# A decoder layer on one core: one activation half's low part moved to an aligned place, small parameters loaded in transposed form, and one chunk's matmuls in plain order

## The chip, the cores and the metric

The kernel runs on one core of one Trainium2 chip. The metric is device time in microseconds (us) of one execution. The engines spoken of are PE (TensorE: matmuls and transposes; PEld is its weight load), ACT (ScalarE), DVE (VectorE), POOL (GpSimd) and SP (SyncE, which here only issues DMAs). Each engine works through its own queue in order; a `behind(...)` in the code only sets where an instruction stands in a queue.

## The reference

One layer of 512 tokens and 1024 columns, float32: half a step of a SwiGLU feed-forward network (FFN1), a token mixer, and half a step of a second one (FFN2), each between two RMS norms:

```
x = x + 0.5 * rms_norm(swiglu_ffn(rms_norm(x, norm_pre[l, 0]), ffn1_w_in[l], ffn1_w_out[l]), norm_post[l, 0])
mixed = token_mixer(rms_norm(x, norm_pre[l, 1]), w_mix_in[l], conv_w[l], conv_b[l],
                    mlstm_gate_bias[l], lower_bounds[l], hgrn_norm[l], mlstm_norm[l], w_mix_out[l])
x = x + rms_norm(mixed, norm_post[l, 1])
x = x + 0.5 * rms_norm(swiglu_ffn(rms_norm(x, norm_pre[l, 2]), ffn2_w_in[l], ffn2_w_out[l]), norm_post[l, 2])
```

`swiglu_ffn` is `(silu(gate) * up) @ w_out` with `gate, up = split(x @ w_in)` and 2816 inner columns. The mixer projects to the inputs of four HGRN2 heads and four mLSTM heads, puts the mLSTM queries and keys through a causal convolution of width 4 (`conv_w`, `conv_b`), runs both recurrences in chunks, norms each head (`hgrn_norm`, `mlstm_norm`) and projects back. `lower_bounds` is the running sum of a softmax over `hgrn_lb_logits`.

## The kernel before, in words

**Precision.** A float32 operand is split in two parts of type fp32r: `hi`, a rounding made on ACT (L289 for weights), and `lo`, the rest, made on DVE (L291). Each product of two operands is three matmuls: hi with hi, hi with lo, lo with hi.

**First matrix of the FFNs.** The 11 pairs of column blocks are each computed from seven products p1 to p7 of half-size operands (a Strassen scheme with shared sums), written out by hand as the lists `HEADS`, `ORDER`, `HEADS2` and `ORDER2`; pair 0 of FFN1 goes by eight plain products c1 to c4 and e1 to e4. A product (`prod`, L621) is 24 matmuls of 128x128 by 128x256. p2 accumulates into the PSUM bank in which p1 stands, after ACT has copied p1's result out of it (L648); p2's matmuls into the bank wait for that copy. What follows a product on ACT or DVE stands in `after`.

**The activation tiles.** The transposed, split activations stand in four tiles `xt[0]` to `xt[3]` (their fp32r views are `xq[n]` or `xh[n]`), each with hi first and lo behind it. In `xt[0]` the lo part that the FFN's products p1, c1 and c3 read stands 16 elements (64 B, `STEP`) off the aligned place `D:2*D`. The sums of activations for p3, p6 and p7 (tiles `sq`) are made in the FFN's head by the steps L392 and L393 (the "turns"), on DVE and ACT in turn.

**The start.** `start` lists the first products of FFN1 and the splits and turns between them, and `small_params` loads the convolution's weights and bias, the logits and the two head norms: five DMAs from SP into 36 rows of a tile `rows` (L1273 to L1277), one PE transpose (L1279), one DVE copy into the tile `prm` (L1280, 128 partitions x 36), and then the softmax for the lower bounds on DVE and ACT (L1283 to L1293, with a table load on ACT at L1286).

**The end of FFN1.** `ffn_out` multiplies by the second matrix chunk by chunk of 128 tokens; the last of the four chunks has an order of its own, which lets one weight place go early ("free") so that the first mixer weight is split (`first_split`) in the middle of the chunk. `head4` then begins the mixer's projection (L561, L550).

Of the kernel before, what the change touches and what calls it, by code (L numbers as in the profile page):

```python
# [118 lines left out]
class Layer:  # L119
# [146 lines left out]
    def split(self):  # L266

        nc = self.nc
        it = self.items.popleft()
        raw = self.raw[it.key]  # L270
        _, a, b = raw.shape
        if it.dst:
            w = it.dst()
        else:
            if self.wt is None:
                self.wt = self.wp.tile([P, 2 * D * WBUF + FRONT + PAD], F32R, name="w")
            if not self.slot and it.key[0] != "mix":
                self.free = deque(FREE2 if it.key[0] == "f2" else FREE)
            n, o = self.lie("out" if it.key[1] == "out" else "mix" if it.key[0] == "mix" and b == 512 else "any")
            self.free.remove(n)  # L280
            w = self.wt[:, o : o + 2 * D].rearrange("p (b k t) -> p b k t", b=2, k=a)
            self.slot[id(w)] = n, o, w
        hi, lo = self.both(w)
        if it.sums:
            raw, hi, lo = (self.flat(v)[:, QUARTER:] for v in (raw, hi, lo))
        self.ready.append((w, it.dst is not None))
        rows = it.rows
        if rows is None:
            self.cast = nc.scalar.copy(hi, raw)  # L289
            yield  # L290
            self.low = nc.vector.tensor_tensor(lo, raw, hi.bitcast(F32), op=ALU.subtract)  # L291
        else:
            for j in range(a):
                nc.scalar.activation(hi[:, j], raw[:, j], AF.Copy, scale=rows[:, j : j + 1])
            yield
            for j in range(a):
                nc.vector.scalar_tensor_tensor(
                    lo[:, j], raw[:, j], rows[:, j : j + 1], hi[:, j].bitcast(F32), op0=ALU.mult, op1=ALU.subtract
                )
        with self.behind(*self.hold):  # L300
            for out, other in it.adds:
# [3 lines left out]
                added = (nc.vector if late else nc.gpsimd).tensor_tensor(o, o, c, op=ALU.add)  # L305
# [206 lines left out]
                stack.enter_context(self.tc.issue_after(i.ins))  # L512
            yield

    def last(self, mm, ys, pieces, g, after, trans, head, out=lambda i: (), cast=False):


        for i in range(NT):
            for left in mm(i):
                if left == "free":  # L520
                    self.first_split = self.split()
                    next(self.first_split)
                    with self.behind(self.cast):
                        after(i - 1)
                elif i == NT - 1 and left == 2:
                    trans(i - 2)
            self.post1(i, *ys[i], pieces(i), g, *out(i))
            if not (cast and i == 2):
                after(i)
            if i == 2:  # L530
                trans(0)
        head(trans)
# [32 lines left out]
    def head4(self, trans, scaled):  # L565
# [2 lines left out]

        self.head = []
        lows = [self.low]  # L570
        for _ in self.first_split:
            pass
        with self.behind(*lows, self.low):
            scaled(2, 0)
        with self.behind(self.added[0]):
# [13 lines left out]
    def open_ffn(self, ctx, second=False):  # L589
# [12 lines left out]
        self.left.update({"e1": xq[2], "e2": xq[3], "e3": xq[2], "e4": xq[3]})  # L602
        self.gs, self.held, self.copies = [], {}, []
        self.hs, self.bank, self.later, self.u, self.had = deque(), {}, deque(), {}, set()

    def prod(self, p, t, feed=True):

# [28 lines left out]
    def after(self, p, t):  # L636
# [23 lines left out]
                gate()  # L660
        elif p == "p5" and t < self.filled:
            u = self.u[t] = self.st("u")
            tt(self.two_by(u), self.two_by(bank["p5", t]), h1, ALU.subtract)
        elif p == "p5":
            q = bank["p6", t] = self.ps()
            tt(self.two_by(q), self.two_by(bank["p5", t]), h1, ALU.subtract)
# [29 lines left out]
    def ffn_head(self, trans):  # L696
# [13 lines left out]
        for n, (p, t) in enumerate(HEADS2):  # L710
# [6 lines left out]
            if n == 0:  # L717
                with self.behind(*norm):
                    trans(2)
            elif n == 2:  # L720
                trans(3)
            elif n in (5, 6, 8, 9):
                for g in self.gs:
                    next(g)
        self.hold = ()
        self.holes()

# [10 lines left out]
    def start(self, gpre):  # L738
# [84 lines left out]
        p12 = prod()  # L823
        e2()
        self.full_split()
        step(g2)
        step(g3)
        p21 = prod()
# [16 lines left out]
    def ffn_in(self):  # L845
# [5 lines left out]
        for n, (p, t) in enumerate(ORDER2[len(HEADS2) :] if self.second else ORDER[len(HEADS) :]):  # L851
# [11 lines left out]
            self.after(p, t)  # L863
            if t == PAIRS - 1 and p in ("p3", "p7"):
                self.hs.append(self.h_tile(len(self.hs)))
        self.feed()
        self.lag()

# [95 lines left out]
    def ffn_out(self, gpost_row, scale, after, trans, head):  # L964
# [140 lines left out]
        def chunk(i):  # L1105
            vn = [(v, n) for v in range(2) for n in range(LF)]
            if i == 0:

                vn.sort(key=lambda f: f[1])
            turns = [(v, LF - 1) for v in range(2)]  # L1110
            if i == NT - 1 and not self.second:

                vn.insert(1, vn.pop(LF))
                turns[0] = vn[LF - 1]
            for v, n in vn:
                plain(C, ws[n], hs[n], i, v, False)
# [9 lines left out]
        self.last(chunk, ys, lambda i: pieces(C, i), g, after, trans, head, lambda i: (self.hf[:, 4 + i, :],), not self.second)  # L1126
        self.holes()


# [135 lines left out]
                    made.append(Item((name, PAIRS - 1, "a"), ()))  # L1265
        return made

    def small_params(self):

        nc = self.nc  # L1270
        mc = self.cp
        rows = self.sp.tile([36, P], F32, tag="junk", bufs=1, name="rows")
        nc.sync.dma_start(rows[0:16, :], self.conv_w[0].rearrange("j (c p) -> (j c) p", p=P))  # L1273
        nc.sync.dma_start(rows[16:20, :], self.conv_b[0].rearrange("(c p) -> c p", p=P))
        nc.sync.dma_start(rows[20:28, :], self.hgrn_lb_logits.rearrange("r (c p) -> (r c) p", p=P))
        nc.sync.dma_start(rows[28:32, :], self.hgrn_norm[0].rearrange("(c p) -> c p", p=P))
        nc.sync.dma_start(rows[32:36, :], self.mlstm_norm[0].rearrange("(c p) -> c p", p=P))  # L1277
        pt = self.ps()
        nc.tensor.transpose(pt[:, :36], rows, self.ident[:36, :36])  # L1279
# [3 lines left out]
        nc.vector.tensor_tensor(mx, l0, l1, op=ALU.max)  # L1283
# [7 lines left out]
        nc.vector.tensor_tensor(self.lb, e0, e1, op=ALU.mult)  # L1291
        self.oml = mc.tile([P, 4], F32, name="oml")
        nc.vector.tensor_scalar(self.oml, self.lb, -1.0, 1.0, op0=ALU.mult, op1=ALU.add)  # L1293

        self.gb = mc.tile([36, 1], F32, name="gb")
        with self.behind(self.pow):
# [677 lines left out]
```

## Time and profile before

| | |
|---|---|
| median of three runs | 930.9 us (930.17 to 931.26) |
| the profiled execution | 929.95 us, its span 928.2 us |
| granted PE clock over the span | 0.999 |
| busy, share of the span | PE 99%, DVE 83%, ACT 56%, POOL 20% |
| the chain that ended last | PE 98%, ACT 1% |

Of the chain, 46% of the span are the FFN products of L621. So the time is first the number of matmuls times the pace of one, and then the few places where PE waits. In the timeline rows, the columns are start, duration (first start to last end of the group), engine, line, operation, output and inputs, shapes and count; a bracket gives the idle time ahead on that engine and what ended it. The end of a matmul is modelled some 0.16 us past the start of the next, so two groups are compared from start to start.

### The profile page before, as it was taken

How to read it: one execution, taken by the hardware profiler on the slowest of the kernel's cores; microseconds unless marked ns; L12 is line 12 of the kernel's file. 1: busy time of each engine (PE TensorE's matmuls, PEld its weight loads, DVE VectorE, ACT ScalarE, POOL GpSimd, SP SyncE). 2: the span in 40 equal slices, each digit the busy share in tenths (PEclk: the TensorE clock that was granted, in tenths of full speed). 3: DMA queues.
4: the chain of work that ended last, by engine and by line, in shares of the span. 5: the costliest groups of instructions: out<-in, count | busy, mean ns of one | idle time of the engine just before them, and what ended most of it. 6: DMA issues, size and time to landing. Idle time of an engine off the chain costs nothing.

```text
span 928.2 us, 18311 instructions
## 1 busy us (share of the span) xinstructions
PE 919.2 (99%) x7429; PEld 886.1 (95%) x7429; DVE 766.8 (83%) x994; ACT 524.2 (56%) x751; POOL 182.6 (20%) x252
## 2 busy tenths in 40 slices
PE   9999999999999999999999999999999999999997
PEld 7999999999999999998887887899999999999997
DVE  6899988889887876698757665799898989998886
ACT  7646455557566467956533445495455455756661
POOL 2531112111111045652321310304000000011002
PEclk9999999999999999999999999999999999999999
DMA  9255888766897834898842124352454435279542
GB/s 311 76 160 136 188 205 199 193 148 159 231 270 227 249 87 121 169 187 190 171 80 69 46 91 140 110 179 62 125 160 134 135 117 161 89 227 249 175 148 91
DMA packets 118768, 145.42 MB, mean 157 GB/s; under 512 B 7414, under 2 KB 91418, under 8 KB 118684
## 3 DMA queue, kind: packets, MB, share of 16 engines
q1 hardware_dynamic: 102716, 129.05, 45.3%
q0 software_dynamic: 15680, 14.69, 12.1%
q8 instruction: 58, 0.95, 0.4%
q10 hardware_dynamic: 288, 0.52, 0.2%
q14 instruction: 26, 0.21, 0.1%
HBM read 142.14 MB, written 31.46 MB: 187 GB/s over the span
## 4 chain that ended last, share of the span: by engine, by line
PE 98%; ACT 1%; DMA 0%; DVE 0%; issue 0%; DVEq 0%; POOLq 0%; POOL 0%; ACTq 0%
PE ps L621 46%; PE ps L1012 14%; PE ps L1004 9%; PE ps L550 6%; PE ps L193 5%; PE ps L195 5%; PE ps L194 5%; PE ps L1443 2%; PE ps L359 1%; PE ps L561 1%; PE ps L1536 0%; PE ps L1741 0%; PE ps L1714 0%; PE ps L1489 0%; DMA hf<-in_norm_pre_dram 0%; PE ps L1738 0%
## 5 line engine op out<-in xcount | busy, mean ns | idle before, releaser
L289 ACT CAST w<-raw 128x1024 fp32r<-128x1024 f32 x246 | 251.2, 1027 | 200.4 <-PE ps L621 90.7
L291 DVE TENSOR_TENSOR w<-raw,w 128x1024 fp32r<-128x1024 f32 x246 | 299.6, 1221 | 31.8 <-ACT w L289 29.9
L621 PE MATMUL ps<-xq,w 128*128 128x256 f32 x2016 | 237.2, 277 | 0.0
L621 PEld LDWEIGHTS ps<-xq,w 128*128 128x128 f32 x2016 | 232.9, 188 | 0.0
L621 PE MATMUL ps<-sq,w 128*128 128x256 f32 x1512 | 177.9, 276 | 0.3
L621 PEld LDWEIGHTS ps<-sq,w 128*128 128x128 f32 x1512 | 174.2, 188 | 0.9 <-ACT ps L672 0.9
L305 DVE TENSOR_TENSOR raw<-raw,raw 128x1024 f32<-128x1024 f32 x72 | 89.9, 1252 | 7.6 <-DMA raw<-in_ffn_w_in_dram 6.1
L1012 PE MATMUL ps<-w,hs 128*128 128x256 f32 x672 | 80.9, 276 | 0.0
L1004 PE MATMUL ps<-w,hs 128*128 128x256 f32 x672 | 79.0, 276 | 0.0
L1012 PEld LDWEIGHTS ps<-w,hs 128*128 128x128 f32 x672 | 78.3, 188 | 0.0
L193 PE MATMUL ps<-w,xq 128*128 128x512 f32 x192 | 77.9, 407 | 0.1
L1004 PEld LDWEIGHTS ps<-w,hs 128*128 128x128 f32 x672 | 77.4, 188 | 0.0
L194 PE MATMUL ps<-w,xq 128*128 128x512 f32 x192 | 74.9, 391 | 0.0
L195 PE MATMUL ps<-w,xq 128*128 128x512 f32 x192 | 74.8, 391 | 0.0
L550 PE MATMUL ps<-xq,w 128*128 128x256 f32 x480 | 57.6, 282 | 0.0
L550 PEld LDWEIGHTS ps<-xq,w 128*128 128x128 f32 x480 | 56.8, 189 | 0.5 <-issue 0.5
L944 POOL DMA_DIRECT2D f2sums<-in_ffn_w_out_dram x15 | 20.9, 1538 | 176.3 <-DMA f2sums<-in_ffn_w_out_dram 176.3
L884 ACT CAST hs<-hf 128x1024 fp32r<-128x1024 f32 x32 | 33.7, 1054 | 28.0 <-PE ps L1012 20.3
L885 DVE TENSOR_TENSOR hs<-hf,hs 128x1024 fp32r<-128x1024 f32 x32 | 39.1, 1223 | 9.0 <-ACT hs L884 8.4
L944 POOL DMA_DIRECT2D f1sums<-f1sums x26 | 22.5, 866 | 110.5 <-DMA f1sums<-in_ffn_w_out_dram 56.4
L193 PEld LDWEIGHTS ps<-w,xq 128*128 128x128 f32 x192 | 36.1, 188 | 8.5 <-issue 1.0
L195 PEld LDWEIGHTS ps<-w,xq 128*128 128x128 f32 x192 | 36.0, 188 | 8.1 <-DVE xq L366 0.3
(275 smaller groups left out, 1216.7 us busy)
## 6 DMA issues: line engine op xcount, KB each, us to landing
raw<-in_ffn_w_in_dram SPq DMA_DIRECT2D x98, 512.0 KB, 5.0
raw<-in_ffn_w_out_dram SPq DMA_DIRECT2D x44, 512.0 KB, 4.9
raw<-in_w_mix_in_dram SPq DMA_DIRECT2D x28, 512.0 KB, 7.5
raw<-f2sums SPq DMA_DIRECT2D x15, 512.0 KB
raw<-f1sums SPq DMA_DIRECT2D x13, 512.0 KB, 7.1
raw<-in_w_mix_out_dram SPq DMA_DIRECT2D x8, 512.0 KB, 3.7
f2sums<-in_ffn_w_out_dram SPq DMA_DIRECT2D x30, 128.0 KB, 5.6
f2sums<-in_ffn_w_out_dram SPq DMA_DIRECT2D x15, 256.0 KB, 5.4
```

The lines of the kernel that those rows point to most:

```text
L193: mm(ps, sh, mh, start=start, stop=False, **kw)
L194: mm(ps, sh, ml, start=False, stop=False, **kw)
L195: mm(ps, sl, mh, start=False, stop=stop, **kw)
L289: self.cast = nc.scalar.copy(hi, raw)
L291: self.low = nc.vector.tensor_tensor(lo, raw, hi.bitcast(F32), op=ALU.subtract)
L305: added = (nc.vector if late else nc.gpsimd).tensor_tensor(o, o, c, op=ALU.add)
L550: mm(ps[:, u0:u1], w[:, a, k, :], self.xop(k, b, u0, u1), start=k + n + m == 0, stop=k == ND - 1 and n == 2, skip_group_check=True,)
L621: self.nc.tensor.matmul(ps[:, c], wb[b][:, k, v], left[d][:, k, :], start=first and a + n + k == 0, stop=n == 2 and k == KH - 1, skip_grou ...
L885: self.nc.vector.tensor_tensor(lo, src, hi.bitcast(F32), op=ALU.subtract)
L944: nc.gpsimd.dma_start(to[:, a:b], v, accum_op=ALU.add)
L1004: mm(out, a[kk][:, i * P : (i + 1) * P], w[:, b, kk, QUARTER * v : QUARTER * (v + 1)], start=begin and c == kk == n == 0, stop=kk == 1 and ...
L1012: mm(ps[:, QUARTER * c : QUARTER * (c + 1)], A[a][:, c], B[b], start=begin and c == n == 0, stop=n == 2, skip_group_check=True,)
```

## The change

Three edits.

1. `low_moves`: two ACT copies of 128x1024 each bring the low part of `xt[0]` to the aligned place `D:2*D`, by way of a free part of `hf` since the two places overlap; from then on p1, c1 and c3 read it there. In FFN1 it stands in `start` behind the split after product e2, in FFN2 in the head after product 12, behind the ACT copy of the p1 before.
2. `small_params`: the five DMAs write straight into `prm`, each a strided transpose of elements of 4 bytes (128x16, 128x4, 128x8, 128x4 and 128x4). The tile of rows, the PE transpose and the DVE copy go. The softmax becomes `lower_bound`, called in `ffn_in` two products later, behind the DVE step of the second p5.
3. The last chunk of FFN1's second matrix goes back to the plain order of the other chunks: no "free", and the first mixer weight is split by `full_split` in `head4`.

```diff
@@ def last
-    def last(self, mm, ys, pieces, g, after, trans, head, out=lambda i: (), cast=False):
+    def last(self, mm, ys, pieces, g, after, trans, head, out=lambda i: ()):
         for i in range(NT):
             for left in mm(i):
-                if left == "free":
-                    self.first_split = self.split()
-                    next(self.first_split)
-                    with self.behind(self.cast):
-                        after(i - 1)
-                elif i == NT - 1 and left == 2:
+                if i == NT - 1 and left == 2:
                     trans(i - 2)
             self.post1(i, *ys[i], pieces(i), g, *out(i))
-            if not (cast and i == 2):
-                after(i)
+            after(i)
@@ def head4
-        for _ in self.first_split:
-            pass
+        self.full_split()
@@ new, behind open_ffn
+    def low_moves(self, j):
+        via = self.hf[:, j : j + 2, :].rearrange("p a t -> p (a t)")
+        for dst, src in ((via, self.xt[0][:, D + STEP : 2 * D + STEP]), (self.xt[0][:, D : 2 * D], via)):
+            self.nc.scalar.copy(dst, src)
+        self.left.update({p: self.both(self.xq[0]) for p in ("p1", "c1", "c3")})
@@ def after
         elif p == "p5" and t < self.filled:
             u = self.u[t] = self.st("u")
-            tt(self.two_by(u), self.two_by(bank["p5", t]), h1, ALU.subtract)
+            self.tick = tt(self.two_by(u), self.two_by(bank["p5", t]), h1, ALU.subtract)
@@ def ffn_head
+            elif n == 12:
+                with self.behind(self.copied):
+                    self.low_moves(8)
@@ def start
         e2()
         self.full_split()
+        self.low_moves(8)
         step(g2)
         step(g3)
@@ def ffn_in
+            if n == 1 and not self.second:
+                self.lower_bound()
@@ def ffn_out
-            turns = [(v, LF - 1) for v in range(2)]
-            if i == NT - 1 and not self.second:
-                vn.insert(1, vn.pop(LF))
-                turns[0] = vn[LF - 1]
...
-                if i == NT - 1 and not self.second and (v, n) == (1, 0):
-                    yield "free"
-                if (v, n) in turns:
+                if n == LF - 1:
                     yield 2 - v
@@ def small_params
-        rows = self.sp.tile([36, P], F32, tag="junk", bufs=1, name="rows")
-        nc.sync.dma_start(rows[0:16, :], self.conv_w[0].rearrange("j (c p) -> (j c) p", p=P))
...
-        pt = self.ps()
-        nc.tensor.transpose(pt[:, :36], rows, self.ident[:36, :36])
-        nc.vector.tensor_copy(self.prm, pt[:, :36])
+        for c, w in (
+            (0, self.conv_w[0].rearrange("j (c p) -> p (j c)", p=P)),
+            (16, self.conv_b[0].rearrange("(c p) -> p c", p=P)),
+            (20, self.hgrn_lb_logits.rearrange("r (c p) -> p (r c)", p=P)),
+            (28, self.hgrn_norm[0].rearrange("(c p) -> p c", p=P)),
+            (32, self.mlstm_norm[0].rearrange("(c p) -> p c", p=P)),
+        ):
+            nc.sync.dma_start(self.prm[:, c : c + w.shape[1]], w)
@@ def lower_bound (new; the softmax that stood in small_params)
+        with self.behind(self.tick):
+            nc.vector.tensor_tensor(mx, l0, l1, op=ALU.max)
```

How it moves instructions. First ACT in the head of FFN1, between the turns that fill `xq_76` (L393) and the copy of product p1 of pair 2 out of its bank, `ps_506` (L648); a row has the line, the operation, output, input and shape. Before:

```order
L643 ACTIVATE hf_113<-ps_415 128x2x256
L289 CAST w<-raw_35_277 128x1024
L393 CAST sq_114<-ps_336 128x4x128
L393 CAST sq_114<-ps_376 128x4x128
L648 COPY hf_113<-ps_506 128x2x256
L289 CAST w<-raw_10_123 128x1024
L650 ACTIVATE hf_113<-ps_386 128x2x256
```

Now:

```order
L643 ACTIVATE hf_113<-ps_415 128x2x256
L289 CAST w<-raw_35_277 128x1024
L603 CAST hf_113<-xq_78 128x1024
L603 CAST xq_78<-hf_113 128x1024
L393 CAST sq_114<-ps_336 128x4x128
L393 CAST sq_114<-ps_376 128x4x128
L648 COPY hf_113<-ps_506 128x2x256
L289 CAST w<-raw_10_123 128x1024
L650 ACTIVATE hf_113<-ps_386 128x2x256
```

The two moves (L603, tile `xq_78` is `xt[0]`) stand three places ahead of the copy L648; nothing else moved there.

On PE at the same place, the last rows of the head before, where the second row accumulates into `ps_506`:

```order
L621 MATMUL ps_445<-xq_77,sq_115 128x256 x24
L621 MATMUL ps_506<-xq_75,w 128x256 x24
L1279 MATMUL ps_635<-ident,rows 128x36
L621 MATMUL ps_670<-xq_76,w 128x256 x24
L621 MATMUL ps_699<-xq_76,w 128x256 x24
```

Now these are the same rows without L1279. In FFN2, the ACT queue around product 12 now reads

```order
L289 CAST w<-raw_644_6729 128x1024
L648 COPY hf_6461<-ps_7108 128x2x256
L603 CAST hf_6461<-xq_78 128x1024
L603 CAST xq_78<-hf_6461 128x1024
L289 CAST w<-raw_6782 128x1024
L650 ACTIVATE hf_6461<-ps_7047 128x2x256
```

where before the two L603 rows were not there. Last, ACT at the end of FFN1, from the hi of the second pair of turned columns (L365) to the second mixer weight. Before:

```order
L289 CAST w<-raw_3740 128x1024
L448 ACTIVATE junk_4115,col_4113<-xs 128x512
L448 ACTIVATE junk_4120,col_4118<-xs 128x512
L365 CAST xq_78<-ps_4138 128x4x128
L365 CAST xq_75<-ps_4145 128x4x128
L448 ACTIVATE junk_4178,col_4176<-ps_3447 128x256
L448 ACTIVATE junk_4184,col_4182<-ps_3448 128x256
L289 CAST w<-raw_3776 128x1024
```

Now:

```order
L448 ACTIVATE junk_4086,col_4084<-xs 128x512
L448 ACTIVATE junk_4091,col_4089<-xs 128x512
L448 ACTIVATE junk_4175,col_4173<-ps_3445 128x256
L365 CAST xq_78<-ps_4135 128x4x128
L365 CAST xq_75<-ps_4142 128x4x128
L289 CAST w<-raw_3738 128x1024
L448 ACTIVATE junk_4181,col_4179<-ps_3446 128x256
L289 CAST w<-raw_3774 128x1024
```

The cast of the first mixer weight (the first L289 row of each) went from ahead of the two square sums (L448) to behind the two L365 casts. The reason stands on PE, where one unit of six matmuls of the last chunk, `ps<-w,hs`, moved behind the four rows `ps<-w,xq`.

More of the change, by code (lines that the diff above doesn't have):

```diff
@@ L288, in split @@
         if rows is None:
-            self.cast = nc.scalar.copy(hi, raw)
+            nc.scalar.copy(hi, raw)
             yield
@@ L1120, in chunk @@
                     add(C, T, 0)
-                if i == NT - 1 and not self.second and (v, n) == (1, 0):
-                    yield "free"
-                if (v, n) in turns:
+                if n == LF - 1:
                     yield 2 - v
-        self.last(chunk, ys, lambda i: pieces(C, i), g, after, trans, head, lambda i: (self.hf[:, 4 + i, :],), not self.second)
+        self.last(chunk, ys, lambda i: pieces(C, i), g, after, trans, head, lambda i: (self.hf[:, 4 + i, :],))
         self.holes()
@@ L1266, in ffn_items, with lower_bound @@
         return made
-    def small_params(self):
-        nc = self.nc
-        mc = self.cp
-        rows = self.sp.tile([36, P], F32, tag="junk", bufs=1, name="rows")
[L1273 to L1277, printed above, removed]
-        pt = self.ps()
-        nc.tensor.transpose(pt[:, :36], rows, self.ident[:36, :36])
-        nc.vector.tensor_copy(self.prm, pt[:, :36])
+    def lower_bound(self):
+        nc, mc = self.nc, self.cp
         l0, l1 = self.prm[:, 20:24], self.prm[:, 24:28]
         mx, e0, e1 = self.col(4), self.col(4), self.col(4)
-        nc.vector.tensor_tensor(mx, l0, l1, op=ALU.max)
+        with self.behind(self.tick):
+            nc.vector.tensor_tensor(mx, l0, l1, op=ALU.max)
         nc.vector.tensor_tensor(e0, l0, mx, op=ALU.subtract)
@@ L1293, in small_params @@
         nc.vector.tensor_scalar(self.oml, self.lb, -1.0, 1.0, op0=ALU.mult, op1=ALU.add)
+    def small_params(self):
+        nc = self.nc
+        mc = self.cp
+        for c, w in (
[6 more added lines that the diff above has]
+            nc.sync.dma_start(self.prm[:, c : c + w.shape[1]], w)
         self.gb = mc.tile([36, 1], F32, name="gb")
```

## The prediction

> **What bounds the kernel now.** I read the page first, its busy times and its chain, then the waits of PE, then the timelines of PE, ACT and DVE around each of the three edits.
>
> ```profile
> PE 919.2 (99%) x7429; PEld 886.1 (95%) x7429; DVE 766.8 (83%) x994; ACT 524.2 (56%) x751; POOL 182.6 (20%) x252
> ...
> PE 98%; ACT 1%; DMA 0%; DVE 0%; issue 0%; DVEq 0%; POOLq 0%; POOL 0%; ACTq 0%
> ...
> PEld ps L621 <- ACT ps L672: 0.9, 3, 0.3
> ```
>
> PE is busy 99% of the span and carries 98% of the chain; in the FFN products PE's weight load waits for a copy of ACT three times, 0.9 us together. So a change can gain only by a faster matmul or fewer of them, and it loses exactly as much as it makes PE wait. The question for each part is which it does.
>
> **The head of FFN1, PE and then ACT.**
>
> ```profile
> 40.13 2.88 PE L621 MATMUL ps<-xq,sq 128*128 128x256 f32 x24
> 42.85 2.88 PE L621 MATMUL ps<-xq,w 128*128 128x256 f32 x24
> 45.67 0.25 PE L1279 MATMUL ps<-ident,rows 36*128 36x36 f32 x1
> 45.85 5.72 PE L621 MATMUL ps<-xq,w 128*128 128x256 f32 x48
> ...
> 51.41 0.28 PE L621 MATMUL ps<-sq,w 128*128 128x256 f32 x1
> ```
>
> ```profile
> 39.68 0.61 ACT L643 ACTIVATE hf<-ps 128x512 f32<-128x512 f32 x1
> 40.16 1.05 ACT L289 CAST w<-raw 128x1024 fp32r<-128x1024 f32 x1
> 41.10 1.08 ACT L393 CAST sq<-ps 128x512 fp32r<-128x512 f32 x2
> 42.06 0.62 ACT L648 COPY hf<-ps 128x512 f32<-128x512 f32 x1
> 42.53 1.09 ACT L289 CAST w<-raw 128x1024 fp32r<-128x1024 f32 x1
> 43.48 0.64 ACT L650 ACTIVATE hf<-ps 128x512 f32<-128x512 f32 x1
> 44.56 0.59 ACT L393 CAST sq<-ps 128x512 fp32r<-128x512 f32 x1 [0.44 <-DVE ps L392]
> 46.07 0.59 ACT L393 CAST sq<-ps 128x512 fp32r<-128x512 f32 x1 [0.93 <-PE ps L1279]
> ```
>
> A product is 42.85 - 40.13 = 2.72 us. The product at 42.85 is p2 of pair 2, which accumulates into the bank that the L648 copy reads; the copy ends at 42.06 + 0.62 = 42.68, 0.17 us ahead of it. ACT has no gap from 39.68 to 44.12, each row begins before the last has drained, so whatever is put ahead of that copy delays it in full. This is the tightest place that the change touches.
>
> **Part 1, the cost.** The two moves stand between the rows at 40.16 and 41.10. They are ACT copies of 128x1024, like the L289 cast: 1.05 us long, the next row 0.94 us after its start. The second move reads what the first writes, so it can't overlap its drain: 1.05 for the first and 0.94 for the second, 2.0 us. The copy then ends at 44.68 instead of 42.68. How soon PE follows such a release, and what it costs to start again, is seen at the one kind of wait that PE has for ACT in these products:
>
> ```profile
> 677.65 0.57 ACT L672 COPY ps<-ps 128x512 f32<-128x512 f32 x1 [2.08 <-PE ps L621]
> ...
> 678.27 5.72 PE L621 MATMUL ps<-sq,w 128*128 128x256 f32 x48
> 683.83 5.04 PE L621 MATMUL ps<-xq,w 128*128 128x256 f32 x43
> ```
>
> The copy ends at 678.22 and PE goes on at 678.27, 0.05 later; the 48 matmuls behind it take 683.83 - 678.27 = 5.56 us instead of 5.44, so 0.12 for the restart. The p2 here would start at 44.73 instead of 42.85: +1.88, and +0.12. Bounds: if ACT ran the two moves without any drain between them and each at the 0.94 pitch, +1.77; if each waited for a semaphore and ran at 1.09 (the longest L289 row here), about +2.2. I take 2.0 with the restart. The later rows of ACT and DVE in this stretch feed products behind that p2, and PE's delay gives them all the same 1.9 us, so I count no second wait; ACT's next idle time, 0.44 us before 44.56 and 0.93 before 46.07, takes up the rest.
>
> **Part 1, the gain.** Where the low part of `xt[0]` stands now, its products are slower than others. Timelines of PE in FFN2 and FFN1:
>
> ```profile
> 691.42 2.94 PE L621 MATMUL ps<-xq,w 128*128 128x256 f32 x24
> 694.19 5.60 PE L621 MATMUL ps<-sq,w 128*128 128x256 f32 x48
> ...
> 707.79 2.88 PE L621 MATMUL ps<-xq,w 128*128 128x256 f32 x24
> 710.51 5.60 PE L621 MATMUL ps<-sq,w 128*128 128x256 f32 x48
> ```
>
> ```profile
> 165.91 8.38 PE L621 MATMUL ps<-xq,w 128*128 128x256 f32 x72
> 174.13 2.88 PE L621 MATMUL ps<-sq,w 128*128 128x256 f32 x24
> ```
>
> The p1 at 691.42 takes 2.77, the p2 at 707.79 (another activation tile) 2.72; the three products from 165.91, a p1 among them, take 8.22 instead of 8.16. So 0.05 to 0.06 us, say 0.055, for each product with this low part. Behind the moves stand eight p1 of FFN1 (pairs 3 to 10) and four of FFN2 (pairs 2, 4, 9 and 10, by the two lists): 12 x 0.055 = 0.66 us. That the aligned place gives 2.72 isn't shown for this tile; the nearest rows are the aligned tiles, all at 2.72. Bounds: 0 and 0.66; I take 0.66.
>
> The Trainium skill, "SBUF — State Buffer", section "Who interferes with whom", gives TensorE two independent read ports, one for the moving operand and one for the weights, and says that PE never waits on anyone. By that rule the place of the low part would change nothing and the sum would be 0.66 us higher; the rows at 691.42 and 707.79 speak against it here.
>
> **Part 1 in FFN2.** There the moves stand behind the L648 copy, in a gap:
>
> ```profile
> 634.16 0.58 ACT L648 COPY hf<-ps 128x512 f32<-128x512 f32 x1
> 638.14 1.05 ACT L289 CAST w<-raw 128x1024 fp32r<-128x1024 f32 x1 [3.40 <-POOL raw L305]
> ```
>
> ACT idles 3.40 us for a sum made on POOL; 2.0 us of moves fit in. Cost 0; if POOL were earlier by 1.4 us or more the cast would come late. The next p1 that reads the new place is pair 2's, the first of those four, well behind.
>
> **Part 2.** The PE row at 45.67 goes. From 42.85 to 51.41 stand 72 matmuls and that row: 8.56 us against 3 x 2.72 = 8.16, so the transpose with its change of weights and back costs 0.40 us, which is saved. The DVE copy at L1280 is off the path. The five strided DMAs and their first reader:
>
> ```profile
> 21.10 1.40 SPq L1273 DMA_DIRECT2D rows<-in_conv_w_dram  x1
> ...
> 28.11 0.36 SPq L160 DMA_DIRECT2D gpost<-in_norm_post_dram  x1
> 54.51 3.82 SPq L250 DMA_DIRECT2D raw<-in_ffn_w_in_dram  x3
> ```
>
> ```profile
> L1518 SPq DMA_DIRECT2D graw<-in_w_mix_in_dram x1: 368/368/368, 349.1 to 349.1; - x1
> ...
> 356.32 0.84 POOL L1525 CAST gw<-graw 128x32 fp32r<-128x32 f32 x2 [4.65 <-DMA graw<-in_w_mix_in_dram]
> ```
>
> 128 x 36 = 4608 pieces of 4 bytes replace 36 rows. The nearest row is `graw`, 1024 rows of 32 bytes, which POOL has 7.2 us after its issue at 349.1. Scaled whole by pieces, 4.5 x 7.2 = 32 us, from 21.1 to 53.5; if only the time above some fixed part scales, much less. On SP nothing is issued from 28.5 to 54.51, so the feed isn't behind them. The first reader is now `lower_bound` on DVE, behind the second p5's step:
>
> ```profile
> 54.49 0.68 DVE L640 TENSOR_TENSOR u<-ps,hf 128x512 f32<-128x512 f32 x1
> ...
> 58.53 0.68 DVE L640 TENSOR_TENSOR u<-ps,hf 128x512 f32<-128x512 f32 x1
> ```
>
> These are the steps of the two p5; the order puts `lower_bound` between and behind them, later than 54.5 plus PE's delay. DMA done by 53.5 at worst: cost 0. Its small DVE rows and the table load on ACT are the same ones as before some us later, beside the same work. Were the DMAs later than that, DVE would stand with the lo splits queued behind it, and PE after some slack.
>
> **Part 3.** Six matmuls change places, none is added.
>
> ```profile
> 333.80 1.05 ACT L289 CAST w<-raw 128x1024 fp32r<-128x1024 f32 x1 [0.77 <-PE ps L1004]
> ...
> 336.27 1.05 ACT L365 CAST xq<-ps 128x512 fp32r<-128x512 f32 x2
> 337.22 0.39 ACT L448 ACTIVATE junk<-ps 128x256 f32<-128x256 f32 x1
> ```
>
> ```profile
> 337.95 0.84 PE L1004 MATMUL ps<-w,hs 128*128 128x256 f32 x6
> 338.63 5.87 PE L561 MATMUL ps<-xq,w 128*128 128x256 f32 x48
> 344.35 1.03 PE L359 MATMUL ps<-ident,xn 128*128 128x128 f32 x8
> ```
>
> The first mixer weight's cast moves from 333.80 to behind the L365 pair, so to about 337.25, and ends at 338.3; PE needs it at 338.63. About 0.3 us remain of nearly 4: cost 0, bounds 0 and 1.0 (another row of ACT or a late place for the weight ahead of it). The 48 matmuls of L561 take 5.72 us, 119 ns each against 113 in the FFNs; since the weight is taken later it may get another place in its pool, and its pace may change by up to 48 x 6 ns = 0.3 either way. I take -0.1.
>
> **The sum.** +2.0 (wait and restart) - 0.66 (12 products) - 0.40 (transpose) - 0.1 (part 3) = +0.84 us. The profiled execution took 929.95, so 930.8; the median is 930.9, which is 0.95 above the profiled execution, and I forecast against the median: 930.9 + 0.84, about 931.8 us.
>
> **Rivals.**
> - No wait in the head: if the copy still got out by 42.85, the rest is a gain of 1.16, 929.7 us. For it: it would hold if the moves took less than the 0.17 us of slack, and a loss turns to a gain once the wait with its restart is under 1.16, which is two moves of some 0.6 us. Against it: both moves stand ahead of the copy in ACT's queue, and ACT has no gap there. 0.07.
> - The place of the low part makes no difference for `xt[0]`, so its 0.66 stays out: 932.4 us. Against it: every product on the aligned tiles is at 2.72. 0.06.
> - The mixer's first weight comes late at 338.63 by about 1 us, since 0.3 us of slack is little: 932.8 us. 0.13.
> - The strided DMAs outlast 55 us and hold DVE at `lower_bound`: each us of a landing past about 57 is then a us that the splits behind it, and PE, come later. A landing at 60 is +3, so 934.8 us; pieces at twice the time of `graw`'s would land at 21 + 64 = 85, and cost far more. Against it: scaled by `graw` they are done by 53.5, and a part of its 7.2 us can't grow with the pieces. 0.08.
>
> **The numbers.** My forecast has 0.60; something else, mostly slower, 0.06. The range 930.2 to 933.6 leaves out the first rival, the last, and part of the rest, 0.2 together. A measurement of this kernel tells about 0.2% from no change, 1.86 us: 929.04 and 932.76. Slower: the last rival, half of the third, the rest, and the upper tail of the forecast, 0.26. Faster: the lower tail of the first rival, 0.04. Same: 0.70.
>
> **What would show it.** In the profile after: on ACT two L603 rows from 41.1 to 43.1, the L648 copy at 44.06, PE's p2 at 44.7 with an entry of PE's weight load waiting for ACT L648, about 1.9 us; no PE row between that p2 and the next product, 2.72 us; the p1 products behind it 2.72 instead of 2.77; the FFN2 moves inside the gap at 634.7. I am wrong if that wait is missing or under 1 us, if DVE idles at the first `prm` reader, or if L561 waits for ACT.

## The result, and the profile after

The changed kernel takes 940.78 us (five runs, 940.26 to 943.47) where the kernel before takes 930.9 (930.17 to 931.59): a ratio of 1.0112, 95% interval 1.0096 to 1.0128, so 9.9 us slower. The forecast was 931.8 with a range of 930.2 to 933.6. In the profiled execution (940.26 us) the span grew from 928.2 to 938.5. Two runs at a lowered granted clock are left out below: one of the ninth experiment (1323 us at 0.65) and one of the kernel before beside it (1021 us at 0.85).

The page of the kernel after has PE as full as before, and the same number of instructions less the transpose; the products of L621 now cost more each:

```profile
PE 928.1 (99%) x7428; PEld 895.0 (95%) x7428; DVE 767.0 (82%) x993; ACT 529.1 (56%) x755; POOL 182.7 (19%) x252
...
L621 PE MATMUL ps<-xq,w 128*128 128x256 f32 x2016 | 240.3, 279 | 1.5 <-ACT hf L648 1.5
L621 PE MATMUL ps<-sq,w 128*128 128x256 f32 x1512 | 181.2, 279 | 0.4
```

Before, the same two groups were:

```profile
L621 PE MATMUL ps<-xq,w 128*128 128x256 f32 x2016 | 237.2, 277 | 0.0
L621 PE MATMUL ps<-sq,w 128*128 128x256 f32 x1512 | 177.9, 276 | 0.3
```

The wait for L648 is there, as forecast. Timelines of ACT and of PE in the head, after:

```profile
39.89 1.05 ACT L289 CAST w<-raw 128x1024 fp32r<-128x1024 f32 x1
40.83 1.06 ACT L603 COPY hf<-xq 128x1024 f32<-128x1024 f32 x1
41.92 1.05 ACT L603 CAST xq<-hf 128x1024 fp32r<-128x1024 f32 x1
42.88 1.06 ACT L393 CAST sq<-ps 128x512 fp32r<-128x512 f32 x2
43.83 0.60 ACT L648 COPY hf<-ps 128x512 f32<-128x512 f32 x1
```

```profile
40.05 2.88 PE L621 MATMUL ps<-xq,sq 128*128 128x256 f32 x24
44.48 8.75 PE L621 MATMUL ps<-xq,w 128*128 128x256 f32 x72 [1.54 <-ACT hf L648]
...
72.85 8.64 PE L621 MATMUL ps<-xq,w 128*128 128x256 f32 x72
81.33 2.99 PE L621 MATMUL ps<-sq,w 128*128 128x256 f32 x24
```

The copy ends at 44.43 and p2 starts at 44.48 instead of 40.05 + 2.72 = 42.77: a wait of 1.71 us. So far the forecast. But the three products from 72.85, 28 us later and waiting for nothing, take 81.33 - 72.85 = 8.48 us instead of 8.22. PE does not come back to its pace before the end of FFN1. Busy times in two windows of 100 us inside FFN1, the kernel before and then after (columns: the window and its length; busy time and, in brackets, instructions of PE, PEld, DVE, ACT and POOL; granted clock, DMA share, GB/s):

```profile
100.00:200.00 100.00, 100.00 (x882) 100.00 (x881) 85.25 (x85) 52.44 (x65) 20.68 (x22) 1.00 0.84 197
200.00:300.00 100.00, 100.00 (x884) 100.00 (x883) 88.71 (x113) 64.91 (x95) 14.05 (x21) 1.00 0.77 208
```

```profile
100.00:200.00 100.00, 100.00 (x851) 100.00 (x851) 79.99 (x79) 50.13 (x61) 20.02 (x22) 1.00 0.81 186
200.00:300.00 100.00, 100.00 (x851) 100.00 (x851) 87.93 (x113) 61.98 (x91) 14.81 (x22) 1.00 0.75 200
```

The granted clock is 1.00 in all four, PE is busy all the time, and yet 851 matmuls go through instead of 882 to 884: 117.5 ns against 113.3. Followed start by start, the matmuls stand at 117.8 ns from 44.70 to 343.38 us, 2536 in a row, and not one of them is at 113.3. In the kernel before such stretches occur too, but in the mixer (47 matmuls of L561 from 338.63 us, 288 of L550 from 351.66 and 125 from 390.52); there the kernel after is the faster one. Timeline of PE at the start of the mixer, after (before, L561 ran from 338.63 to 344.35):

```profile
350.82 5.67 PE L555 MATMUL ps<-xq,w 128*128 128x256 f32 x48
356.34 1.03 PE L359 MATMUL ps<-ident,xn 128*128 128x128 f32 x8
```

The 48 take 5.52 us here and 5.72 before. So the account, by PE's starts against the kernel before: +1.63 us at the p2 of the head, +12.19 at the last transposes of FFN1 (335.02 and 347.21), +10.35 in the mixer (399.00 and 409.35), +10.28 at the end.

I call the two paces the fast rhythm (113.3 ns) and the slow one (117.8 ns). The experiments ask what puts PE in the slow rhythm and what ends it.

### The profile page after: what moved, and what is told of

Same layout as the page of the kernel before. It is cut to its first block, busy times and chain, and to the rows that moved or that the text cites. A ratio compares the mean times of both kernels' runs of the same rounds, so it can differ in the third digit from the quotient of the medians.

```text
span 938.5 us, 18307 instructions
## 1 busy us (share of the span) xinstructions
PE 928.1 (99%) x7428; PEld 895.0 (95%) x7428; DVE 767.0 (82%) x993; ACT 529.1 (56%) x755; POOL 182.7 (19%) x252
## 4 chain that ended last, share of the span: by engine, by line
PE 94%; ACT 2%; DMA 1%; DVE 1%; issue 0%; SPq 0%; DVEq 0%; ACTq 0%; POOLq 0%; POOL 0%
PE ps L621 43%; PE ps L1018 14%; PE ps L1010 9%; PE ps L544 6%; PE ps L193 5%; PE ps L195 5%; PE ps L194 5%; PE ps L1446 2%; PE ps L555 1%; PE ps L359 1%; DMA raw<-in_ffn_w_in_dram 1%; DMA xs<-in_x_dram 0%; DVE ps L392 0%; ACT w L289 0%; PE ps L1539 0%; PE ps L1744 0%
## 5 line engine op out<-in xcount | busy, mean ns | idle before, releaser
L289 ACT CAST w<-raw 128x1024 fp32r<-128x1024 f32 x246 | 251.5, 1027 | 207.1 <-PE ps L621 101.2
L621 PE MATMUL ps<-xq,w 128*128 128x256 f32 x2016 | 240.3, 279 | 1.5 <-ACT hf L648 1.5
L621 PEld LDWEIGHTS ps<-xq,w 128*128 128x128 f32 x2016 | 236.0, 188 | 1.7 <-ACT hf L648 1.7
L621 PE MATMUL ps<-sq,w 128*128 128x256 f32 x1512 | 181.2, 279 | 0.4
L621 PEld LDWEIGHTS ps<-sq,w 128*128 128x128 f32 x1512 | 177.4, 188 | 1.1 <-ACT ps L672 0.9
L1018 PE MATMUL ps<-w,hs 128*128 128x256 f32 x672 | 82.3, 278 | 0.0
L1010 PE MATMUL ps<-w,hs 128*128 128x256 f32 x672 | 80.8, 279 | 0.0
L1018 PEld LDWEIGHTS ps<-w,hs 128*128 128x128 f32 x672 | 79.7, 188 | 0.0
L1010 PEld LDWEIGHTS ps<-w,hs 128*128 128x128 f32 x672 | 79.0, 188 | 0.0
L891 DVE TENSOR_TENSOR hs<-hf,hs 128x1024 fp32r<-128x1024 f32 x32 | 39.1, 1222 | 10.3 <-ACT hs L890 9.9
```

Of the source, the lines that this page charges most:

```text
L621: self.nc.tensor.matmul(ps[:, c], wb[b][:, k, v], left[d][:, k, :], start=first and a + n + k == 0, stop=n == 2 and k == KH - 1, skip_grou ...
L891: self.nc.vector.tensor_tensor(lo, src, hi.bitcast(F32), op=ALU.subtract)
L1010: mm(out, a[kk][:, i * P : (i + 1) * P], w[:, b, kk, QUARTER * v : QUARTER * (v + 1)], start=begin and c == kk == n == 0, stop=kk == 1 and ...
L1018: mm(ps[:, QUARTER * c : QUARTER * (c + 1)], A[a][:, c], B[b], start=begin and c == n == 0, stop=n == 2, skip_group_check=True,)
```

## The experiments

All times are medians; the kernel before took 930.6 to 930.8 beside them.

**1. The moves without the wait.** In the changed kernel, `low_moves` goes behind the p2.

```diff
         e2()
         self.full_split()
-        self.low_moves(8)
...
         p22()
+        self.low_moves(8)
```

> The changed kernel with the two moves of FFN1 placed behind the p2 of pair 2 instead of ahead of its copy, so that PE doesn't wait in the head. Theory A (the wait breaks PE's rhythm, and what starts behind a break runs at 117.8 ns per matmul until something ends it): with no break the matmuls of FFN1 stay at 113.3 ns and the whole kernel takes about 929.8 us, 1.1 under the kernel before. Rival B (the slow pace comes from the program itself, from the row that is gone from PE or from where instructions and data lie now, and not from the wait): still about 939 us, and 117.8 ns behind 45 us.

Measured: 928.14 us, ratio 0.9973 (0.9961 to 0.9984); six of the seven runs lie between 927.6 and 930.3, one at 944.82. In the profiled run the fast rhythm holds to the end of FFN1, and a little better than before, since p1 now reads the aligned place; the first of the two windows:

```profile
100.00:200.00 100.00, 100.00 (x885) 100.00 (x884) 85.22 (x85) 53.09 (x66) 20.65 (x22) 1.00 0.82 194
```

So neither the missing transpose nor the place of the low part is enough to make FFN1 slow: in six of seven runs it isn't, and rival B falls. The single run at 944.8 has no profile; by its time, 16.7 us more, the slow rhythm can still come here without the wait. The gain is also larger than the 1.1 us expected; the eighth experiment shows where the rest comes from.

**2. The moves alone on the kernel before.** `low_moves` and its call in `start` are added to the kernel before.

```diff
         e2()
         self.full_split()
+        self.low_moves(8)
```

> The kernel before with the two moves of FFN1 alone, at the place of the change; the transpose of the parameters on PE stays, one product behind the waiting p2, and the last chunk stays. Both see a wait of about 1.7 us. Theory A, if a transpose on PE ends the slow rhythm: one product at 117.8 ns, then 113.3 again, about 930.9 + 1.9 - 0.44 (eight p1 at 2.72) = 932.4 us. Theory A, if the slow rhythm outlasts the transpose: about 942. Rival B, the row gone from PE: the row is here, so 932.4 as well, and only the first run tells A from B.

Measured: of ten runs two at 931.3 and 931.9, eight from 942.7 to 945.9. The same program does the one or the other. The profiled run (945.93, the slowest of the ten) is slow from 49.83 to 345.69 us, 2512 matmuls, although the transpose of L1287 stands behind the p2: that transpose doesn't end the slow rhythm. In FFN2, where the low part was not moved, the same profile has a slow stretch from 690 us on that ends at 709 us, behind the low-part matmuls of a p1. This run showed one thing more, the granted clock behind the wait (0.51 and 0.50 in the last two windows):

```profile
42.80:44.84 2.04, 0.27 (x3) 0.07 (x1) 2.04 (x3) 2.04 (x5) 0.07 (x1) 1.00 0.00 0
44.84:46.10 1.26, 1.26 (x10) 1.26 (x11) 1.26 (x3) 1.26 (x2) 0.00 (x0) 1.00 0.04 13
46.10:48.90 2.80, 2.80 (x16) 2.80 (x14) 2.80 (x5) 2.15 (x4) 1.34 (x1) 0.51 0.02 6
48.90:49.50 0.60, 0.60 (x4) 0.30 (x3) 0.38 (x1) 0.16 (x1) 0.60 (x1) 0.50 0.00 0
```

**3. The transpose put back.** The changed kernel with the rows, the transpose and the copy of the kernel before.

```diff
-            nc.sync.dma_start(self.prm[:, c : c + w.shape[1]], w)
+        nc.sync.dma_start(rows[0:16, :], self.conv_w[0].rearrange("j (c p) -> (j c) p", p=P))
...
+        nc.tensor.transpose(pt[:, :36], rows, self.ident[:36, :36])
+        nc.vector.tensor_copy(self.prm, pt[:, :36])
```

> The changed kernel with the parameters loaded in rows again and transposed on PE, all else as changed. Theory A with a transpose that ends the slow rhythm: about 932 us (930.9 + 1.9 wait and restart - 0.66 for the low part - 0.1). Theory A without that: about 941. Theory C (the strided DMAs are what slows FFN1, by traffic or by where they leave the queues): 932 as well, with no slow product behind the wait at all, where A sees the product behind the wait at 117.8 ns.

Measured: ten runs, two at 929.1 and 929.5, two at 935.7 and 935.9, five from 940.0 to 941.0, one at 946.7. So the strided DMAs aren't the cause (theory C falls), and a transpose isn't a cure. The profiled run is one of the two near 936: fast in FFN1, and slow in FFN2 to the end. The slow rhythm begins at 768.05 us, behind a wait for a weight (L289) and a DVE step (L640); it goes on behind the next wait, for L672, and lasts from 772.0 us for 1319 matmuls. Two windows, ahead of it and inside:

```profile
740.00:765.00 25.00, 24.91 (x220) 24.71 (x219) 20.53 (x21) 12.55 (x16) 0.00 (x0) 1.00 0.37 113
775.00:800.00 25.00, 25.00 (x214) 25.00 (x214) 23.12 (x27) 13.76 (x20) 0.00 (x0) 1.00 0.41 127
```

**4. Half the wait, low part not moved in FFN1.** One copy into a free part of `hf` instead of the two moves.

```diff
-        self.low_moves(8)
+        self.nc.scalar.copy(self.hf[:, 8:10, :].rearrange("p a t -> p (a t)"), self.xt[0][:, D + STEP : 2 * D + STEP])
```

> The changed kernel with one ACT copy of 128x1024 into a free part of hf in place of the two moves in the head of FFN1; p1 of FFN1 goes on reading the low part at its old place, so the result is the same. PE waits about 0.8 us instead of 1.8. If any wait of this kind leaves PE in the slow rhythm, 117.8 ns up to 343 us of the timeline and about 940 us. If the length of the wait or the chance of a start decides, it may fall to 113.3 ns after two to four matmuls, as behind the waits of FFN2: 930.9 + 0.9 + 0.1 - 0.40 - 0.2 (four p1 of FFN2) = 931.3 us.

Measured: 930.07 us, seven runs from 929.2 to 931.8, three from 934.6 to 935.8, none near 940. The wait was 0.55 us. The profiled run is slow behind the wait from 43.65 us, and then fast from 74.05 on. What stands there is the p1 of pair 3, from 71.69 us on, whose low part lies at the old place: behind its eight low-part matmuls the pace is the fast one. In the kernel before every pair from 1 on has such a p1; in the changed kernel none behind the wait has. That is theory D, and the run left two explanations, the shorter wait and the old place. The three runs near 935 have no profile. In this kernel FFN2's low part is moved, as in the third experiment, whose profile lost 1319 x 4.5 ns = 5.9 us there; they fit a slow rhythm in FFN2 alone.

**5. The whole wait, nothing moved.** Two copies of the same size into free parts of `hf`, and no `low_moves` in either FFN.

```diff
-        self.low_moves(8)
+        via, nxt = (self.hf[:, j : j + 2, :].rearrange("p a t -> p (a t)") for j in (8, 10))
+        self.nc.scalar.copy(via, self.xt[0][:, D + STEP : 2 * D + STEP])
+        self.nc.scalar.copy(nxt, via)
...
-            elif n == 12:
-                with self.behind(self.copied):
-                    self.low_moves(8)
```

> The changed kernel with the same two ACT copies in the head of FFN1, but into free parts of hf, and no moves in either FFN: p1, c1 and c3 read the low part at its old place, 64 B off, all the way. PE waits as in the changed kernel, about 1.7 us. Theory D (a break can leave PE in a slow rhythm of 117.8 ns, and a product that reads the low part at the old place ends it, which is why the kernel before never stayed in it): slow from 44.5 us to the first p1 behind it, pair 3's at 70 to 75 us, at most 250 matmuls x 4.5 ns = 1.1 us, and fast from there in every run: 929.5 to 932, none near 940. Theory A without that (only breaks end it): most runs near 939 to 941.

Measured: 931.45 us, ratio 1.0009 (0.9999 to 1.0018), nine runs from 929.6 to 932.3 and one at 934.1, none near 940. The wait in the profile is 1.4 us. Behind it 258 matmuls are slow, up to 74.92 us, inside the p1 of pair 3 again; before and behind that p1, in two windows of 22 us:

```profile
50.00:72.00 22.00, 22.00 (x189) 22.00 (x189) 21.82 (x28) 10.18 (x12) 8.20 (x3) 1.00 0.61 192
76.00:98.00 22.00, 22.00 (x196) 22.00 (x196) 21.17 (x24) 11.29 (x13) 0.81 (x1) 1.00 0.57 152
```

189 matmuls against 196, where 22 us hold 187 at 117.8 ns and 194 at 113.3, and the window's edges add one or two. In FFN2 of the same run, a slow stretch that goes on behind a wait for L672 (772.96 us) ends at 788.64 after 133 matmuls, where another p1 with the low part at the old place runs; in the third experiment, where FFN2's low part had been moved, the like stretch ran to the end.

The ending is no accident of these places. Followed start by start through all thirteen profiles of this case (the kernel before, the changed one and the eleven experiments), PE went into the eight low-part matmuls of a product at the old place 41 times in the slow rhythm, and it came out in the fast one all 41 times. The other direction occurs too, but only at the very first such product, near 12 us: four profiles go in fast there and come out slow. Every slow stretch of more than nine matmuls ends at such a product, at a pause in the stream or at the end of the program.

**6. One old p1, then the aligned place.** The wait as in the fifth, and `low_moves` behind the p1 of pair 3, so that one product reads the old place behind the wait and seven the aligned one.

```diff
+            if (p, t) == ("p5", 3) and not self.second:
+                self.low_moves(12)
```

> The wait in the head as in the changed kernel (two copies into free places), and the low part brought to the aligned place only behind the p1 of pair 3: one product of 24 matmuls reads it at the old place behind the wait, the other seven p1 of FFN1 at the aligned one; no moves in FFN2. Theory D: that one product ends the slow rhythm, and no later product starts it, so FFN1 is fast from 75 to 331 us: 929 to 932 us, where the changed kernel took 940.8 with the same wait. If it isn't the odd place that ends it: about 940.

Measured: 930.93 us, ratio 1.0006 (0.9997 to 1.0016), six runs from 930.3 to 931.0 and four from 932.1 to 933.3. None is near 940, with a wait of 1.3 us (1.7 in the changed kernel) and the p1 places of the changed kernel behind 75 us. The two clusters are about 1.5 us apart; 258 slow matmuls more make 258 x 4.5 ns = 1.2 us, so they fit a start in the fast or in the slow rhythm, ended by the one old p1. The profile of this kernel shows a start in the fast rhythm, so it does not show the ending itself; the profiles of the second (FFN2), fourth, fifth and tenth experiments do.

**7. No moves at all.** Parts 2 and 3 alone.

```diff
-        self.low_moves(8)
...
-            elif n == 12:
-                with self.behind(self.copied):
-                    self.low_moves(8)
```

> The changed kernel without any low_moves: parts 2 and 3 alone. Theory D: no run stays slow, since each p1 ends the slow rhythm; 930.8 - 0.4 (transpose gone) - 2.1 (the mixer's 460 matmuls of L561 and L550 that ran at 118 before now at 113.3) = 928.3 us, all runs within 1.5 us. If the fast mixer of the first runs came from the moves and not from part 3: 930.4.

Measured: 929.05 us, ratio 0.9981 (0.9972 to 0.999), all ten executions from 928.0 to 929.6: none in which the slow rhythm lasted, as theory D has it. PE has no wait in the head here, so this run alone doesn't test the ending.

**8. Part 3 alone on the kernel before.**

```diff
-                if i == NT - 1 and not self.second and (v, n) == (1, 0):
-                    yield "free"
-                if (v, n) in turns:
+                if n == LF - 1:
                     yield 2 - v
```

(with the rest of the last chunk's order as in the change)

> The kernel before with the last chunk of FFN1 in plain order, part 3 alone. Theory E (the first mixer weight lay 64 B off before, its matmuls run at 120 ns and leave PE in the slow rhythm up to the next break; split later it lies at an aligned place): L561 and L550 from 338 to 405 us at 113.3 instead of 118 ns, -2.1 us, less up to 0.4 for a wait of the first weight: 928.7 to 929.1. If part 3 only moves work: 930.8.

Measured: 928.84 us, ratio 0.9978 (0.9969 to 0.9988), ten runs from 928.2 to 929.1. Part 3 is worth -1.8 us. Beside the seventh it also says that part 2 is worth nothing by the median, though its trace shows the gain of the transpose: the seventh kernel's PE is 0.15 us ahead of this one's before the transpose and 0.52 us behind it, a gain of 0.37. The gain goes at 766.6 us of FFN2, where the seventh kernel's PE waits for a weight and this one's doesn't, and both start the next product at the same time. Timelines of PE, with part 2 and then without:

```profile
761.34 5.04 PE L621 MATMUL ps<-xq,w 128*128 128x256 f32 x43
766.63 2.97 PE L621 MATMUL ps<-sq,w 128*128 128x256 f32 x24 [0.26 <-ACT w L289]
```

```profile
761.82 5.04 PE L614 MATMUL ps<-xq,w 128*128 128x256 f32 x43
766.70 2.88 PE L614 MATMUL ps<-sq,w 128*128 128x256 f32 x24
```

**9. The first mixer weight alone at the odd place.** In the compiled programs the first mixer weight begins at element 16 of the weights' tile before, and at element 96 in the change; all other weights of these matmuls lie where element 96 does, modulo 512 B. Here the seventh kernel gets that one weight back to 16; the order of all instructions stays. What the expectation calls 64 B off is 64 B from the tile's start; from element 96 it is 80 elements, 320 B.

```diff
+            if it.key == ("mix", 0):
+                o = 16
             self.free.remove(n)
```

> The changed kernel without any moves, and the first mixer weight alone put back 64 B off, at the place that it had before (element 16 of the weights' tile instead of 96); order and everything else as in that run. Theory E (a weight at the odd place runs at 119 to 120 ns and leaves PE in the slow rhythm behind it): 48 matmuls of L555 and 288 of L544 from about 351 to 385 us at 118 ns, +1.6 to +2.1, 930.7 to 931.1 us. If part 3's gain came from the order of the last chunk: 929.05 and 113.3 ns.

Measured: 931.23 us, nine runs from 930.8 to 932.0: 2.2 us above the seventh. In the window of the mixer, the seventh kernel and then this one:

```profile
352.00:386.00 34.00, 34.00 (x303) 34.00 (x302) 22.09 (x35) 30.26 (x34) 21.75 (x38) 1.00 0.57 126
```

```profile
352.00:386.00 34.00, 34.00 (x291) 34.00 (x290) 21.25 (x35) 29.39 (x33) 20.59 (x38) 1.00 0.55 123
```

Only the first 24 of these matmuls use that weight, at 119 to 120 ns. They follow matmuls at 113 ns without any pause, and the slow rhythm goes on behind them through 288 in a row, as it did in the kernel before, and a further 125 behind 391 us. So part 3's gain is the place of one weight, not the order of the chunk.

The addresses in the compiled programs, modulo 512 B, say what "place" can mean. In nearly all of these matmuls the moving operand lies at 160 and the weight at 480, 320 apart. The low part at the old place makes it 224 and 480, 256 apart; this weight makes it 160 and 160, 0 apart. Both odd cases run at 118 to 120 ns on average. Whether the place of each operand counts or the distance between the two isn't shown.

**10. Four copies.** As the fifth, with four copies, for the price of a longer wait.

```diff
         self.nc.scalar.copy(nxt, via)
+        self.nc.scalar.copy(via, nxt)
+        self.nc.scalar.copy(nxt, via)
```

> As the run with two copies into free places and the low part unmoved, but with four copies: PE waits about 3.4 us instead of 1.5. If the wait costs only itself and its restart: 931.45 + 1.95 = 933.4 us. If a longer wait also halves the clock behind it, as in the profile of the moves alone on the kernel before (0.51 for 2.8 us): 934.8 or more, with a stretch of matmuls at 213 ns in the profile.

Measured: 936.38 and 935.34 us, 4.4 above the fifth for 2.2 us more of ACT's work (two copies at 1.08). The weight load waits 4.0 us. The clock is halved from 1.1 us before PE starts again, and behind that for 5.8 us more, 27 matmuls instead of 51:

```profile
45.50:46.60 1.10, 0.00 (x1) 0.01 (x1) 1.00 (x2) 1.10 (x4) 0.00 (x0) 0.50 0.00 0
46.60:52.40 5.80, 5.80 (x27) 5.80 (x28) 4.64 (x8) 3.68 (x6) 2.39 (x1) 0.51 0.02 4
```

The Trainium skill, "TensorE: Matmul & The Clock Gate", section "Part 1: The HAM clock gate", has the clock at half rate after an idle window of about 3.4 us. The wait of the four copies, 3.9 us from the starts of the matmuls around it, is longer than that, and the clock was halved. In the second experiment's profile a wait of 1.9 us was already enough, and there the measurement counts, though it is one run, the slowest of ten; in the profiles of the changed kernel (1.7 us) and of the fifth (1.4 us) the clock stayed at 1.00. The slow rhythm outlasts the halved clock here too, and ends at 79 us, behind the low part of the p1 of pair 3.

**11. The moves behind the p1 of pair 3, no wait.** Parts 2 and 3, FFN1's moves where ACT has time, none in FFN2.

```diff
+            if (p, t) == ("p5", 3) and not self.second:
+                with self.behind(self.copied):
+                    self.low_moves(12)
```

> The changed kernel with the moves of FFN1 put behind the p1 of pair 3, in ACT's idle time, and none in FFN2: PE doesn't wait in the head, the p1 of pair 3 reads the old place and ends whatever slow rhythm the transposes of the start left, and seven p1 read the aligned place. Theory D: every run fast; 929.05 - 7 x 0.055 = 928.7 us, or 929.05 if FFN2 waits for its weights at 766 us and gives the gain back. None of the 940 kind. If the aligned place itself breeds the slow rhythm, some runs are near 940.

Measured: 928.56 us, ratio 0.9976 (0.9966 to 0.9985), all ten runs from 927.5 to 929.1. It is the best of the kernels in which the slow rhythm never lasted, 12.2 us under the changed kernel and 2.1 under the kernel before, and half a microsecond under the seventh, about what the seven aligned p1 should give; that difference alone is within the spread of the runs.

## Why the prediction was wrong

Point by point, by its own steps:

- **The wait in the head** was right. Forecast 1.88 us, measured 1.71, at the place and for the instruction named; the moves' pitches were 1.09 and 0.96 us against 1.05 and 0.94.
- **"so 0.12 for the restart"** is the step that failed, and with it the premise that the kernel "loses exactly as much as it makes PE wait". It was read from the wait of L672, behind which PE comes back to 113.3 ns after two or three matmuls. Behind the head's wait PE stayed at 117.8 ns for 2536 matmuls: 2536 x 4.5 ns = 11.4 us in place of 0.12. The same trace had stretches of 288 and 125 slow matmuls in the mixer, and I had put the 119 ns of L561 down to that weight's place only, without asking why the rows behind it were slow as well.
- **The low part's gain**, 0.66 us: the aligned place does run at 113.3 ns (885 matmuls in 100 us against 882). But the sum held the place of the low part for a cost only. The old place cost 0.055 us a product, and it also ended the slow rhythm, which the second, fourth, fifth and tenth experiments show; with it gone, nothing before the transposes of L359 at 343 us did.
- **The transpose**, -0.40: by the traces of the seventh and eighth experiments it gains 0.37, but the median doesn't move, since FFN2 gives it back in a wait for a weight. The forecast had checked no later wait.
- **Part 3, -0.1**: mis-sized. The bound of 0.3 us either way counted 48 matmuls; by the ninth experiment the place of that weight is worth 2.2 us and by the eighth part 3 gains 1.8.
- **The strided DMAs** were right: the last was issued at 29.6 us and landed 2.9 us later, so all was there by 33 us, well within the bound of 53.5. **FFN2's moves** were hidden as forecast: ACT's idle time ahead of the next cast shrank from 3.40 to 1.37 us.
- **The rivals**: none held a lasting change of pace. The Trainium skill, "SBUF — State Buffer", section "Who interferes with whom", says that PE waits on no one and reads through two independent ports. It does not speak of places; the rival that the prediction drew from it, by which a place would change nothing, fails in the ninth experiment too, where the place of one weight cost 2.2 us.

The sum with measured terms, for a run that stays slow: +1.7 (wait) + 11.4 (slow rhythm in FFN1) - 0.4 (transpose) - 1.8 (mixer) = 10.9, less the 0.44 us that eight p1 at the old place had cost before: 10.5, against 10.3 in the two spans.

What stays open: which start falls into the slow rhythm. By their times, all five runs of the changed kernel did in FFN1, and eight and six of ten in the second and third experiments, with waits in their profiles from 0.9 to 1.9 us. The length of the wait doesn't decide: in the profiles PE came out slow behind 0.55 us (the fourth) and fast behind 1.3 us (the sixth). It isn't chance alone either, since behind some pauses every profile does the same: the 24 matmuls of L561 between the transposes of L359 (345.13 us in the kernel before) are slow in all thirteen. Nor is it shown what inside PE the two rhythms are. What the runs show is that operands at the odd places start or end them, and that PE may come out of a pause in either.

## What to carry to other kernels

Where PE is the bound, count matmuls per window and compare windows before trusting a constant pace: a clock of 1.00 and a PE at 100% hid 4% over 300 us. A wait of PE costs its length and whatever pace the stream takes up behind it, so a copy that can go elsewhere should not stand ahead of one that PE waits for. And a misplaced operand that looks like a small cost can be holding something in order: move it, and run the kernel ten times rather than three, since the loss may come in some runs only.

## What the runs showed of the hardware

- PE has two steady paces for the same 128x256 matmuls at a granted clock of 1.00, 113.3 and 117.8 ns; it stayed in the slow one for up to 2536 in a row.
- It may come out of a pause (a wait, or a transpose in between) in the slow one. Behind some pauses it is back at 113 ns after two to four matmuls (678.27 us of the kernel before), behind others it stays slow (44.48 us of the changed kernel).
- A moving operand 64 B off its usual place ended the slow pace (at 74.05 us in the fourth experiment, 74.92 and 788.64 in the fifth); a weight 320 B off its usual place started it without a pause (351.66 us before, 352.11 in the ninth experiment).
- A wait of 1.9 us was once enough for the clock to be halved (second experiment), from 1.3 us behind the restart on and for 3.4 us; the longest wait, 3.9 us from the starts of the matmuls around it (tenth experiment), had it halved for 6.9 us, 5.8 of them behind the restart.
